# A first token tile's latent attention dealt into the expert groups of the second

## The chip, the cores and the metric

The kernel runs on one core of a Trainium2 chip. The metric is the time of one execution on the device in microseconds (us), all inputs starting in HBM. The core has TensorE (PE in the profile; PEld is its weight load), VectorE (DVE), ScalarE (ACT), GpSimd (POOL) and SyncE (SP), which run independently and wait for one another on semaphores. Each takes its own instructions in order. SP and POOL here mostly issue DMAs; one memory, SBUF, holds the tiles, and TensorE writes its sums to PSUM, eight banks of 128 x 512 fp32.

## The reference

Two transformer blocks run on 256 tokens of width 1024, all in fp32. Block one is adaptive normalisation, a mixer (gated linear attention beside sliding-window attention) and PEER, a layer of 16,384 experts of one neuron each. Block two is a latent attention (DSA), an MLP, shared keys and values, a sparse attention and a second MLP. The change concerns PEER and DSA:

```python
# PEER, for each token: 8 heads x 16 experts
s1, s2 = q1 @ keys_1.T, q2 @ keys_2.T                 # 128 scores each
v1, i1 = top_k(s1, 16); v2, i2 = top_k(s2, 16)
sc, ci = top_k(v1[:, None] + v2[None, :], 16)         # 16 of 256 pairs
experts, gates = e1 * 128 + e2, softmax(sc)
a = gelu(h . u_tab[experts])                          # one dot of 1024 per expert
out = sum(gates * a * v_tab[experts])                 # weighted rows of 1024
x = rms_norm(x + gate2 * out, final_g)                # end of block one
# DSA, on h = rmsnorm(x, g_attn)
c_q, c_kv, k_idx, w_idx = split(h @ w_in)             # 256, 128, 64, 8 columns; three normed
score = sum_h w_idx[h] * relu(q_idx[h] . k_idx)       # causal
sel = top_k(score, 64)
logits = q_abs . c_kv[sel] + rel_bias;  p = softmax(logits)
x = x + (p @ c_kv[sel]) @ w_uv @ w_o
```

A token tile is 128 tokens; causal order means that the first tile's queries see only the first tile's keys, and the second's see both.

## The kernel before

**Weights.** `weight_order` lists the big weight matrices in tiles of 128 x 1024 in the order of their use. `fetch` issues their loads on SP into a ring of four raw tiles; `prefetch` splits each into two fp32r parts, hi (ACT, line 94) and lo (DVE, line 255), and a product of split operands is three matmuls (`mm3`, lines 260 to 262, and `moving_step`, line 314). `whole_weight` hands out a raw tile unsplit, for an fp32 matmul, which the profile records as two. A second ring, `big`, is there from the latent attention on.

**Experts** (`experts`, lines 732 to 832). The two token tiles have eight groups each, one per head, a group being 16 experts for every one of 128 tokens. For each expert slot `gather` (line 743) issues an indirect DMA on POOL that brings 128 rows of 8 KB, u and v of one expert per token, into one of ten `uv` tiles. DVE takes the dot of u with h (line 815), ACT the gelu (819), DVE multiplies by the gate (805), ACT makes a diagonal matrix of the weights (753), and TensorE adds diagonal times v into two PSUM banks (755). Gelu, weights and outputs go in batches of four slots; a batch is weighed two slots after its last dot. The routing of group n + 1 (`route`, 15 steps on DVE) is dealt into the slots of group n, and all 16 gathers of group n + 1 are put into POOL's queue at slot 8 of group n (slot 0 of the first), where they wait for free tiles. The gate row gate2, a product of eight tiles of `w_gate2`, is made at the start; its eight loads (line 768) use four `uv` tiles, and the 16 query weight tiles run between.

**Latent attention** (lines 1011 to 1246) starts when both token tiles are through the experts. `block_end` forms x + gate2 * out for four halves (lines 348, 349), transposes it, splits it with the norm's gain (189, 190) and multiplies by `a_w_in`. `latents` norms the latents, transposes them, and forms the absorbed query weight from `a_w_uq` and `a_w_uk` (1021). Then come query projections (1157), index scores (1176 to 1182), eight rounds of maximum and replace for each query tile (1187, 1188), the threshold (1190), logits with the bias (1201, 1203), softmax (`add_max` 992, 980, 987), transposes, values (1227), heads (1234), and the product with `a_w_o`, three matmuls per pair (314), added to x (333). The order of the last part is the string of line 1243. DVE and ACT are kept in program order in the experts and in the first part (`manual_schedule`).

Of the kernel before, what the change touches and what calls it, by code (L numbers as in the profile page):

```python
# [26 lines left out]
EXPERT_TILES = 10  # L27
ROUTED = 8
# [4 lines left out]
def weight_order():  # L33
# [3 lines left out]
    o += [("w_out", (k,), 1024) for k in W_OUT_ORDER] + [("w_peer_q", (j,), 1024) for j in range(16)]  # L37
    mlp = lambda l: ([("w_up", (l, j), 1024) for j in range(32)] + [("w_down", (l, k), 1024) for k in range(32)])
    o += [("a_w_in", (k,), 912) for k in range(4)] + [("a_w_o", (k,), 1024) for k in range(8)] + mlp(0)
# [6 lines left out]
class Kernel:  # L46
# [7 lines left out]
    def __init__(self, ctx, tc, ins):  # L54
# [12 lines left out]
        self.first_big = [p[:2] for p in self.order].index(("a_w_o", (1,)))  # L67
# [19 lines left out]
    def prefetch(self, count, later=None):  # L87

        self.fetch(count)
        while len(self.made) < min(self.used + count, len(self.order)):  # L90
            (pool, raw), self.raw[len(self.made)] = self.raw[len(self.made)], None
            hi, lo = (pool.tile([P, 1024], F32R, name=f"w_{s}", tag=f"w_{s}", bufs=3) for s in ("hi", "lo"))
            cols = raw.shape[-1]
            self.nc.scalar.copy(hi[:, :cols], raw)  # L94
# [16 lines left out]
    def whole_weight(self, name, *idx):  # L111

        n = self.used
        assert self.order[n][:2] == (name, idx) and len(self.made) == n, (self.order[n], name, idx)
        self.fetch(1)
        (_, w), self.raw[n] = self.raw[n], None
        self.made.append(None)
# [614 lines left out]
    def experts(self, pool, gpool, hT, h_nat):  # L732
# [5 lines left out]
        junk = pool.tile([P, D], F32, name="expert_junk")  # L738
        po = {}

        def gather(idx, s):
            uv = pool.tile([P, 2 * D], F32, name="uv", tag="uv", bufs=EXPERT_TILES)
            nc.gpsimd.indirect_dma_start(out=uv, out_offset=None, in_=uv_rows,  # L743
                                         in_offset=bass.IndirectOffsetOnAxis(ap=idx[:, s:s + 1], axis=0))
            return uv

        def outputs(tt, first, last, uvs, w):

            if first:
                po[tt] = [self.ps() for _ in range(2)]  # L750
            for i, uv in enumerate(uvs):
                d = pool.tile([P, P], F32, name="diag_w", tag="diag_w", bufs=4)
                nc.scalar.activation(d, self.ident, AF.Copy, scale=w[:, i:i + 1])  # L753
                for h in range(2):
                    nc.tensor.matmul(po[tt][h], d, uv[:, D + h * 512:D + (h + 1) * 512], start=first and i == 0,  # L755
                                     stop=last and i == len(uvs) - 1)

        with tc.manual_schedule(engines={mybir.EngineType.DVE, mybir.EngineType.Activation, mybir.EngineType.Pool}):
            queries, route = self.route(pool, hT)
            groups = [(tt, h) for tt in range(2) for h in range(8)]  # L760
            routes = {0: route(*groups[0])}
            rows, sums = [], [self.ps() for _ in range(2)]
            spread = pool.tile([P, 2 * D], F32, name="uv", tag="uv", bufs=EXPERT_TILES)[:, :D].rearrange("p (k t) -> p k t", t=P)
            nc.scalar.copy(spread, self.c_cols[:, :, None].to_broadcast([P, KC, P]))
            for k in range(0, KC, 2):
                t = pool.tile([P, 2 * D], F32, name="uv", tag="uv", bufs=EXPERT_TILES)
                for i in range(2):
                    nc.sync.dma_start(t[:, i * D:(i + 1) * D], ins["w_gate2"][k + i])
                rows.append(t)
                if k < 6:  # L770
                    next(queries)

            def gate_products(k):
                for i in range(2):
                    for h in range(2):
                        nc.tensor.matmul(sums[h], spread[:, k + i], rows[k // 2][:, i * D + h * 512:i * D + (h + 1) * 512],  # L776
                                         start=(k + i == 0), stop=(k + i == KC - 1))

            for _ in routes[0][1]:
                pass  # L780
            uvs = {0: [gather(routes[0][0]["idx"], s) for s in range(SLOTS)]}
            routes[1] = route(*groups[1])
            for n in range(4):
                next(queries)
                gate_products(2 * n)
                for _ in itertools.islice(routes[1][1], 0 if n < 2 else 4):
                    pass
            for n, _ in enumerate(routes[1][1]):
                if n % 4 == 3:
                    next(queries)  # L790
            for n in range(len(groups)):
                more = n + 1 < len(groups)
                if n and more:
                    routes[n + 1] = route(*groups[n + 1])
                tt = groups[n][0]
                state, a = routes[n][0], pool.tile([P, SLOTS], F32, name="expert_a", bufs=3)
                act = pool.tile([P, SLOTS], F32, name="expert_act", bufs=3)
                w = pool.tile([P, SLOTS], F32, name="expert_w", bufs=3)
                mine = uvs.pop(n)
                starts = [0, 4, 8, 10, 12, 13, 14, 15] if not more else [0, 4, 8, 12]  # L800
# [3 lines left out]
                def weigh(c):  # L804
                    nc.vector.tensor_tensor(out=w[:, c], in0=act[:, c], in1=state["gate"][:, c], op=ALU.mult)  # L805
                    outputs(tt, n % 8 == 0 and c.start == 0, n % 8 == 7 and c.stop == SLOTS, mine[c], w[:, c])

# [786 lines left out]
```

## Time and profile before

| | us |
|---|---|
| median of three runs (lowest to highest) | 1507.04 (1505.14 to 1511.24) |
| the profiled execution | 1506.71 |
| its span, first to last instruction | 1504.9 |
| first gather issued | 179.16 |
| last dot of the experts ends | 886.4 |
| last addition of the latent attention ends | 978.6 |
| TensorE busy, over the span | 1312.5 (87%) |
| VectorE busy | 977.9 (65%) |
| ScalarE busy | 567.8 (38%) |
| GpSimd busy | 322.6 (21%) |

An engine's busy time says how long it worked, not whether anything waited for it. The span divides by what limits it: up to some 155 us the mixer, to 886 the experts, to 979 the latent attention, then MLP, sparse attention and MLP. The granted clock (PEclk) is TensorE's, as a share of 2.4 GHz, averaged over the stretch. In a row of a stretch the times stand in the order PE, PEld, DVE, ACT, POOL, each with its number of instructions, then PEclk, the share of time that the 16 DMA engines were busy, and GB/s.

### The profile page before, as it was taken

Reading aid. Unit: us, or ns where it says so; the run is one execution under the profiler, and the core shown is the slowest. Engines: PE = TensorE matmul, PEld = TensorE weight load, DVE = VectorE, ACT = ScalarE, POOL = GpSimd, SP = SyncE. Lnnn points to the kernel's source line nnn. Section 1 sums busy time; section 2 is a strip of 40 time slices with the busy share of each in tenths; the row PEclk is TensorE's granted clock in tenths of the full one; section 3 lists DMA queues with packets and bytes.
Section 4 is the critical chain, followed back from the end, with each engine's and each line's share of the span. In section 5 each row is a group of like instructions: output and inputs, shape, how many; then the busy total and the mean of one; then the engine's idle time right before and its main releaser. Section 6 shows DMA issues by size and latency. Waiting matters only on the chain.

```text
span 1504.9 us, 17588 instructions
## 1 busy us (share of the span) xinstructions
PE 1312.5 (87%) x5972; PEld 909.2 (60%) x5972; DVE 977.9 (65%) x2107; ACT 567.8 (38%) x1093; POOL 322.6 (21%) x282
## 2 busy tenths in 40 slices
PE   5999898777877777877787798999999999999998
PEld 5887784333333333323332356699988898799886
DVE  5798765666667666666666557666545777566543
ACT  2544542222222221222222146565434565465432
POOL 0001214444544445434443430000000000000000
PEclk9999999789889899888988899999999999999999
DMA  9867799999999999999999980455555582255550
GB/s 359 304 203 271 269 366 355 400 402 399 383 408 413 410 408 405 381 392 392 409 364 401 414 319 33 168 171 187 186 185 175 182 280 84 99 183 185 190 170 28
DMA packets 83653, 426.41 MB, mean 283 GB/s; under 512 B 10171, under 2 KB 13036, under 8 KB 50668
## 3 DMA queue, kind: packets, MB, share of 16 engines
q0 software_dynamic: 36864, 268.45, 44.2%
q1 hardware_dynamic: 45372, 154.74, 30.1%
q10 hardware_dynamic: 1328, 2.10, 0.4%
q8 instruction: 48, 0.79, 0.2%
q14 instruction: 41, 0.34, 0.1%
HBM read 422.63 MB, written 2.62 MB: 283 GB/s over the span
## 4 chain that ended last, share of the span: by engine, by line
PE 47%; DMA 16%; issue 16%; DVE 9%; POOL 9%; ACT 2%; POOLq 0%; SPq 0%; DVEq 0%; ACTq 0%
PE ps L314 16%; DMA uv<-in_peer_uv,idx 15%; POOL uv L743 8%; PE ps L260 7%; PE ps L262 7%; PE ps L261 7%; DVE expert_junk L815 3%; PE ps L755 3%; PE ps L410 2%; PE ps L776 1%; POOL rstd_r L138 1%; PE ps L1397 1%; DMA w_raw<-in_w_in_a 1%; PE ps L590 1%; DVE w_lo L255 1%
## 5 line engine op out<-in xcount | busy, mean ns | idle before, releaser
L755 PE MATMUL ps<-uv,diag_w 128*128 128x512 f32 x1024 | 515.4, 666 | 148.4 <-ACT diag_w L753 148.3
L755 PEld LDWEIGHTS ps<-uv,diag_w 128*128 128x128 f32 x1024 | 215.2, 215 | 447.3 <-issue 257.4
L815 DVE SCALAR_TENSOR_TENSOR expert_junk<-uv,h_nat 128x1024 f32<-128x1024 f32 x256 | 313.2, 1223 | 213.0 <-DMA uv<-in_peer_uv,idx 212.7
L255 DVE TENSOR_TENSOR w_lo<-w_raw,w_hi 128x1024 fp32r<-128x1024 f32 (+1 forms) x220 | 268.2, 1222 | 212.0 <-ACT w_hi L94 211.9
L743 POOL DMA_INDIRECT uv<-in_peer_uv,idx x256 | 302.1, 1180 | 419.0 <-PE ps L755 340.8
L94 ACT CAST w_hi<-w_raw 128x1024 fp32r<-128x1024 f32 (+1 forms) x220 | 230.0, 1049 | 261.5 <-PE ps L314 141.7
L260 PE MATMUL ps<-hT_hi,w_hi 128*128 128x256 f32 x728 | 207.3, 287 | 1.1 <-ACT hT_hi L189 1.0
L261 PE MATMUL ps<-hT_lo,w_hi 128*128 128x256 f32 x728 | 205.5, 283 | 1.0 <-DVE hT_lo L190 1.0
L262 PE MATMUL ps<-hT_hi,w_lo 128*128 128x256 f32 x728 | 204.5, 281 | 0.0
L753 ACT ACTIVATE diag_w<-ident,expert_w 128x128 f32<-128x128 f32 x256 | 87.3, 393 | 275.0 <-DVE expert_w L805 224.7
L261 PEld LDWEIGHTS ps<-hT_lo,w_hi 128*128 128x128 f32 x728 | 137.4, 189 | 3.6 <-DVE hT_lo L190 2.2
L260 PEld LDWEIGHTS ps<-hT_hi,w_hi 128*128 128x128 f32 x728 | 136.6, 188 | 3.5 <-ACT hT_hi L189 1.9
L262 PEld LDWEIGHTS ps<-hT_hi,w_lo 128*128 128x128 f32 x728 | 137.5, 189 | 0.2 <-DVE w_lo L255 0.2
L819 ACT ACTIVATE expert_act<-expert_a 128x4 f32<-128x4 f32 (+2 forms) x68 | 13.9, 205 | 228.6 <-DVE expert_junk L815 228.5
L314 PE MATMUL ps<-w_hi,u_lo 128*128 128x512 f32 x256 | 81.9, 396 | 0.0
L314 PE MATMUL ps<-w_lo,u_hi 128*128 128x512 f32 x256 | 81.7, 395 | 0.0
L314 PE MATMUL ps<-w_hi,u_hi 128*128 128x512 f32 x256 | 81.6, 395 | 0.0
L138 POOL TENSOR_TENSOR rstd_r<-fin_ms,mhalf 128x1 f32<-128x1 f32 x2 | 1.5, 739 | 326.5 <-DVE fin_ms L1476 326.5
L138 POOL TENSOR_TENSOR rstd_r<-x_ms,mhalf 128x2 f32<-128x2 f32 (+1 forms) x4 | 3.3, 835 | 293.3 <-DVE x_ms L158 293.3
L314 PEld LDWEIGHTS ps<-w_hi,u_lo 128*128 128x128 f32 x256 | 48.2, 188 | 11.4
L314 PEld LDWEIGHTS ps<-w_lo,u_hi 128*128 128x128 f32 x256 | 48.1, 188 | 11.5
L314 PEld LDWEIGHTS ps<-w_hi,u_hi 128*128 128x128 f32 x256 | 47.9, 188 | 11.4
(346 smaller groups left out, 1583.4 us busy)
## 6 DMA issues: line engine op xcount, KB each, us to landing
w_raw<-in_w_up SPq DMA_DIRECT2D x64, 512.0 KB, 3.4
w_raw<-in_w_down SPq DMA_DIRECT2D x64, 512.0 KB, 3.3
w_ada<-in_w_ada SPq DMA_DIRECT2D x40, 512.0 KB, 5.7
w_raw<-in_w_peer_q SPq DMA_DIRECT2D x16, 512.0 KB, 9.4
w_raw<-in_cmp_w SPq DMA_DIRECT2D x16, 512.0 KB, 4.1
w_raw<-in_b_w_in SPq DMA_DIRECT2D x9, 512.0 KB, 5.4
w_raw<-in_w_in_a SPq DMA_DIRECT2D x8, 512.0 KB, 9.0
w_raw<-in_w_in_m SPq DMA_DIRECT2D x8, 512.0 KB, 7.8
```

The costliest lines, as they stand in the source:

```text
L94: self.nc.scalar.copy(hi[:, :cols], raw)
L138: self.nc.gpsimd.tensor_tensor(out=r[:, :n], in0=v, in1=self.mhalf[:, :n], op=ALU.pow)
L255: return self.nc.vector.tensor_tensor(out=lo, in0=src, in1=hi.bitcast(F32), op=ALU.subtract)
L260: nc.tensor.matmul(out, lhsT[0], rhs[0], start=start, stop=False)
L261: nc.tensor.matmul(out, lhsT[0], rhs[1], start=False, stop=False)
L262: nc.tensor.matmul(out, lhsT[1], rhs[0], start=False, stop=stop)
L314: self.nc.tensor.matmul(p[tt][h], x[a][:, tt * P:(tt + 1) * P], w[b][:, h * 512:(h + 1) * 512], start=(kk == 0 and a == 0 and b == 0), sto ...
L410: nc.tensor.matmul(out[j // 2][:, j % 2], w[:, j * P:(j + 1) * P], f, start=(k == 0 and j % 2 == 0), stop=(k == KC - 1 and j % 2 == 1))
L743: nc.gpsimd.indirect_dma_start(out=uv, out_offset=None, in_=uv_rows, in_offset=bass.IndirectOffsetOnAxis(ap=idx[:, s:s + 1], axis=0))
L753: nc.scalar.activation(d, self.ident, AF.Copy, scale=w[:, i:i + 1])
L755: nc.tensor.matmul(po[tt][h], d, uv[:, D + h * 512:D + (h + 1) * 512], start=first and i == 0, stop=last and i == len(uvs) - 1)
L815: nc.vector.scalar_tensor_tensor(junk, mine[s][:, :D], 1.0, h_nat[:, tt], op0=ALU.mult, op1=ALU.mult, accum_out=a[:, s:s + 1])
```

## The change

Nine `uv` tiles instead of ten; the dot is written over the u half of its own tile. A group is weighed in batches of two (the last group ends in single slots), each at the slot after its second dot. Gathers are issued one at a time: nine at the start, then one behind each dot. Routing is no longer tied to the next group: `advance` does one and two steps per slot in turn, through all 16 groups, and a group's index and gate tiles are kept (16 each). The `w_gate2` tiles, `a_w_uq` and `a_w_uk` go through the weight ring unsplit; the absorbed weight is formed in group 1.

Once all groups are routed (`n >= 8 and not waiting`), the routing's memory is given back and `latent_tile(0, ...)`, a generator of some 40 steps that does the whole latent attention of one token tile up to the heads, is advanced one step per slot. `latent_tile(1, ...)` runs after the experts, and between its steps `fill` puts the first tile's product with `a_w_o` (`latent_out`). That product is fp32 with whole weights, loaded into tiles of their own (`wo`). The gain of the norm is put into the two parts of `a_w_in` (`gained_parts`), which is therefore loaded and split once per token tile; the product x * final_g moves from POOL to DVE. The big ring is opened after the latent attention.

```diff
-EXPERT_TILES = 10
-ROUTED = 8
+EXPERT_TILES = 9
+WHOLE = ("w_in_a", "w_gate2", "a_w_uq", "a_w_uk")
...
+    o += [("w_gate2", (k,), 1024) for k in range(8)] + [("w_peer_q", (j,), 1024) for j in range(2, 16)]
+    o += [("a_w_uq", (i,), 1024) for i in range(2)] + [("a_w_uk", (), 1024)]
-    o += [("a_w_in", (k,), 912) for k in range(4)] + [("a_w_o", (k,), 1024) for k in range(8)] + mlp(0)
+    o += [("a_w_in", (k,), 912) for _ in range(2) for k in range(4)] + mlp(0)
...
+    def gained_parts(self, raw, hi, lo, k):
+        for kk in range(2):
+            s, g = slice(kk * 456, (kk + 1) * 456), self.end_gain[:, 0, k + kk:k + kk + 1]
+            self.nc.scalar.activation(hi[:, s], raw[:, s], AF.Copy, scale=g)
+            self.nc.vector.scalar_tensor_tensor(lo[:, s], raw[:, s], g, hi[:, s].bitcast(F32), op0=ALU.mult, op1=ALU.subtract)
...
+            def advance(count=1000, upto=len(groups)):
+                while count and len(routed) < upto:
+                    state, steps = waiting[0]
+                    if next(steps, "end") == "end":
+                        waiting.pop(0)
+                        routed.append(state)
+                    else:
+                        count -= 1
...
+            for _ in range(2):
                 next(queries)
+            sums = [self.ps() for _ in range(2)]
+            for k in range(KC):
+                w = self.whole_weight("w_gate2", k)
+                for h in range(2):
+                    nc.tensor.matmul(sums[h], spread[:, k], w[:, h * 512:(h + 1) * 512], start=(k == 0), stop=(k == KC - 1))
+            advance(upto=1)
+            for _ in range(EXPERT_TILES):
+                gather()
...
-                starts = [0, 4, 8, 10, 12, 13, 14, 15] if not more else [0, 4, 8, 12]
+                starts = [0, 2, 4, 6, 8, 10, 12, 13, 14, 15] if final else list(range(0, SLOTS, 2))
...
+                if n >= 8 and shadow is None and not waiting:
+                    front.close()
+                    shadow = shadow_of(po[0], gate2)
                 for s in range(SLOTS):
                     if n == 0:
                         next(queries, None)
+                    if n == 1 and s == 4:
+                        absorbed()
+                    if final and s == 4:
+                        self.prefetch(3)
+                    if shadow is not None:
+                        next(shadow, None)
+                    else:
+                        advance(1 + s % 2)
+                    if weighed < len(batches) and batches[weighed].stop <= s:
+                        weigh(batches[weighed])
+                        weighed += 1
+                    u = uvs[n * SLOTS + s][:, :D]
+                    nc.vector.scalar_tensor_tensor(u, u, 1.0, h_nat[:, n // 8], op0=ALU.mult, op1=ALU.mult,
                                                    accum_out=a[:, s:s + 1])
...
+                    if len(uvs) < total:
+                        advance(upto=len(uvs) // SLOTS + 1)
+                        gather()
...
+            wo = [self.load(opool, ins["a_w_o"][k], [P, D], f"a_w_o{k}") for k in range(KC)]
+            self.fetch(4)
+            out0, out1 = self.latent_out(0, wo), self.latent_out(1, wo)
+            for _ in self.latent_tile(1, x_mid, po, gate2, h_nat[:, 0], lambda n: list(itertools.islice(out0, n))):
+                pass
+            for _ in out0:
+                pass
+            self.prefetch(2)
+            for _ in out1:
+                pass
...
+    def latent_tile(self, tt, x_old, po, gate2, final_g, fill=lambda n: None):
...
+            for h, s in halves:
+                self.gated_add(pool, xp[:, s], xp[:, s], po[h], gate2[:, s])
+                for k in range(4):
+                    nc.tensor.transpose(ps[h][:, k], xp[:, (4 * h + k) * P:(4 * h + k + 1) * P], self.ident)
+                yield
...
+            for h, s in halves:
+                self.split(ps[h], hT[0][:, 4 * h:4 * h + 4], hT[1][:, 4 * h:4 * h + 4])
+                yield
+                for k2 in range(2 * h, 2 * h + 2):
+                    hi, lo = self.weight("a_w_in", k2, last=True)
...
+            rn, rx = self.power(ms, 1), self.power(var, 1)
+            yield
...
+            nc.vector.tensor_scalar(sl, sl, eps, None, op0=ALU.add)
+            r = self.power(sl, 3)
+            yield
...
+            for _ in range(8):
+                m8 = self.small.tile([P, 8], F32, name="idx_m8")
+                nc.vector.max(out=m8, in_=keep)
+                nc.vector.match_replace(out=keep, in_to_replace=m8, in_values=keep, imm_value=-3e38)
+                yield
...
+                yield from softmax(0)
+                yield
+                transposed(0, nc.scalar.copy)
+                yield from softmax(4)
+                fill(1)
+                yield
+                values(0)
+                fill(1)
+                yield
+                heads_out(0, nc.scalar.copy)
+                transposed(4, nc.vector.tensor_copy)
...
+    def latent_out(self, tt, wo):
+        p = [self.ps() for _ in range(2)]
+        steps = itertools.product(range(KC), range(2)) if tt == 0 else ((c, h) for h in range(2) for c in range(KC))
+        for c, h in steps:
+            self.nc.tensor.matmul(p[h], self.oT[:, c, tt * P:(tt + 1) * P], wo[c][:, h * 512:(h + 1) * 512],
+                                  start=(c == 0), stop=(c == KC - 1))
```

## Rows read from the trace of the kernel before

**Rows 1.** Stretches: us; busy us (instructions) by engine; PEclk, DMA share, GB/s.
```profile
155.00:262.00 107.00, 101.12 (x564) 74.04 (x562) 69.88 (x154) 42.11 (x78) 28.05 (x25) 0.97 0.88 342
262.00:874.00 612.00, 467.53 (x922) 194.92 (x923) 402.98 (x1018) 132.63 (x349) 273.18 (x231) 0.87 0.99 399
...
886.00:979.00 93.00, 84.54 (x400) 64.83 (x399) 64.60 (x194) 53.71 (x118) 8.28 (x8) 0.98 0.34 121
```

**Rows 2.** The page's chain that ended last, shares by engine.
```profile
PE 47%; DMA 16%; issue 16%; DVE 9%; POOL 9%; ACT 2%; POOLq 0%; SPq 0%; DVEq 0%; ACTq 0%
```

**Rows 3.** Groups by form, 270 to 870 us: busy, mean ns | idle.
```profile
L755 PE MATMUL ps<-uv,diag_w 128*128 128x512 f32 x911 | 462.8, 670 | 137.9 <-ACT diag_w L753 137.8
L815 DVE SCALAR_TENSOR_TENSOR expert_junk<-uv,h_nat 128x1024 f32<-128x1024 f32 x228 | 279.0, 1223 | 196.4 <-DMA uv<-in_peer_uv,idx 196.2
L743 POOL DMA_INDIRECT uv<-in_peer_uv,idx x227 | 269.1, 1185 | 336.9 <-PE ps L755 294.2 <-issue 13.8 <-DVE expert_junk L815 8.4
```

**Rows 4.** Waits, 262 to 874 us: total us, times, longest.
```profile
POOL uv L743 <- PE ps L755: 296.1, 153, 10.1
...
DVE expert_junk L815 <- DMA uv<-in_peer_uv,idx: 198.2, 179, 3.5
```

**Rows 5.** Timeline of GpSimd: start, duration, operation [idle before].
```profile
262.09 1.78 POOL L743 DMA_INDIRECT uv<-in_peer_uv,idx  x1 [0.76 <-PE ps L755]
...
873.98 0.94 POOL L743 DMA_INDIRECT uv<-in_peer_uv,idx  x1 [0.38 <-PE ps L755]
```

**Rows 6.** DMA queues (packets, MB, share) and issues (count, us to landing).
```profile
q0 software_dynamic: 36864, 268.45, 44.2%
...
uv<-in_peer_uv,idx POOLq DMA_INDIRECT x256, 9.8
```

**Rows 7.** The chain by time: start, us, what; two TensorE runs.
```profile
172.07 3.43 PE ps L776 x8
...
963.87 13.36 PE ps L314 x57
```

**Rows 8.** Stretches, columns as in the first group: a well supplied one, two clocks.
```profile
480.00:520.00 40.00, 30.73 (x63) 12.48 (x61) 27.01 (x69) 7.93 (x21) 17.42 (x16) 0.88 1.01 417
...
861.00:865.00 4.00, 3.95 (x5) 1.85 (x6) 2.10 (x3) 0.88 (x3) 0.00 (x0) 0.50 1.02 424
865.00:889.00 24.00, 24.00 (x57) 10.48 (x56) 11.86 (x26) 5.97 (x19) 6.75 (x6) 0.99 0.94 375
```

**Rows 9.** Timeline of SyncE's DMA issues: start, duration, what.
```profile
208.37 10.69 SPq L84 DMA_DIRECT2D w_raw<-in_a_w_in  x4
...
234.56 0.43 SPq L967 DMA_DIRECT2D bias<-bias_dram  x1
...
814.56 0.43 SPq L123 DMA_DIRECT2D wqi<-in_a_w_q_idx  x1
```

**Rows 10.** Groups by form in the tail, 886 to 979 us.
```profile
L255 DVE TENSOR_TENSOR w_lo<-w_raw,w_hi 128x1024 fp32r<-128x1024 f32 x13 | 15.5, 1222 | 9.9 <-ACT w_hi L94 9.9
...
L314 PE MATMUL ps<-w_hi,hT_hi 128*128 128x512 f32 x32 | 11.5, 419 | 0.0
...
L190 DVE SCALAR_TENSOR_TENSOR hT_lo<-ps,end_gain,hT_hi 128x256 fp32r<-128x256 f32 x8 | 3.8, 481 | 3.5 <-ACT hT_hi L189 3.5
```

**Rows 11.** Timeline of VectorE, the ends of the tail's stages.
```profile
885.18 1.23 DVE L815 SCALAR_TENSOR_TENSOR expert_junk<-uv,h_nat 128x1024 f32<-128x1024 f32 x1 [1.85 <-DMA uv<-in_peer_uv,idx]
...
906.91 0.63 DVE L1025 COPY lat_raw<-ps 128x456 f32<-128x456 f32 x1 [1.73 <-PE ps L262]
...
913.31 0.69 DVE L1052 COPY latT<-ps 128x512 f32<-128x512 f32 x1 [0.62 <-PE ps L1051]
...
927.08 0.62 DVE L1187 MAX8 idx_m<-score 128x8 f32<-128x128 f32 x2
...
936.47 0.42 DVE L1190 TENSOR_SCALAR score<-score 128x128 f32<-128x128 f32 x2
...
977.94 0.69 DVE L333 TENSOR_TENSOR x_res<-x_res,ps 128x512 f32<-128x512 f32 x1 [0.71 <-PE ps L314]
```

More of the change, by code (lines that the diff above doesn't have):

```diff
@@ L93, in prefetch @@
             cols = raw.shape[-1]
+            if name == "a_w_in":
+                self.gained_parts(raw, hi, lo, 2 * idx[0])
+                self.made.append((hi, lo))
+                continue
             self.nc.scalar.copy(hi[:, :cols], raw)
@@ L729, in swa_steps, with experts, gather @@
             yield
-    def experts(self, pool, gpool, hT, h_nat):
+    def experts(self, pool, gpool, front, hT, h_nat, absorbed, shadow_of):
         nc, ins, tc = self.nc, self.ins, self.tc
         uv_rows = ins["peer_uv"]
-        junk = pool.tile([P, D], F32, name="expert_junk")
         po = {}
-        def gather(idx, s):
+        groups = [(tt, h) for tt in range(2) for h in range(8)]
+        total = len(groups) * SLOTS
+        uvs = []
+        rp = front.enter_context(tc.tile_pool(name="routes", bufs=1, reuse_waits="tile"))
+        def gather():
+            n, s = divmod(len(uvs), SLOTS)
@@ L765, in experts @@
[L765 to L777, printed above, removed]
@@ L791, in experts @@
-            for n in range(len(groups)):
[L792 to L799, printed above, removed]
-                starts = [0, 4, 8, 10, 12, 13, 14, 15] if not more else [0, 4, 8, 12]
+            queries, route = self.route(rp, pool, hT)
@@ new lines, in experts @@
+            for _ in range(2):
+                next(queries)
+            sums = [self.ps() for _ in range(2)]
[6 more added lines that the diff above has]
+                gather()
+            for n in range(5):
+                next(queries)
+                advance(0 if n < 3 else 4, 2)
@@ new lines, in run @@
+        with pool("rows", side="right") as rows:
+            po, gate2 = self.experts(rows, gpool, front, hT, h_nat, lambda: self.absorbed(w_abs), begin)
+        with pool("a_w_o", side="right") as opool, tc.manual_schedule(
+                engines={mybir.EngineType.DVE, mybir.EngineType.Activation}):
+            wo = [self.load(opool, ins["a_w_o"][k], [P, D], f"a_w_o{k}") for k in range(KC)]
[7 more added lines that the diff above has]
+            for _ in out1:
+                pass
@@ L1237, in weights_ready @@
-            def weights_ready(n):
-                with tc.issue_after(done[n].ins), tc.issue_after(projected.ins):
-                    self.prefetch(5)
-            ops = {"S": softmax, "T": transposed, "V": values, "U": heads_out, "W": lambda n: next(steps), "P": weights_ready}
-            steps = self.moving_steps("a_w_o", range(KC), oT, self.add_to_x)
-            for o in "S1 T1 S0 V1 T0 S3 V0 U0 S2 P0 T3 W0 V3 T2 W1 V2 W2 U4 W3".split():
-                ops[o[0]](int(o[1]))
-            for _ in steps:
-                pass
+                        nc.vector.scalar_tensor_tensor(keep, rl[:, i], widx[:, h:h + 1], prev, op0=ALU.mult, op1=ALU.add)
@@ new lines, in latent_tile @@
+                        prev = keep
+                    yield
+            for h0 in (0, 4):
+                nc.scalar.activation(qa[:, h0:h0 + 4], proj(self.w_abs, h0), AF.Copy, scale=float(128.0 ** -0.5))
+                yield
+            for i in range(8):
+                nc.tensor.matmul(logits[i], qa[:, i], latT[:, 2, :S], start=False, stop=(i % per == per - 1))
+            fill(2)
+            yield
+            for _ in range(8):
+                m8 = self.small.tile([P, 8], F32, name="idx_m8")
+                nc.vector.max(out=m8, in_=keep)
+                nc.vector.match_replace(out=keep, in_to_replace=m8, in_values=keep, imm_value=-3e38)
+                yield
@@ new lines, in latent_out @@
+    def latent_out(self, tt, wo):
[4 more added lines that the diff above has]
+                                  start=(c == 0), stop=(c == KC - 1))
+            if c == KC - 1:
+                if tt == 0 and h == 0:
+                    continue
+                for i in range(2) if tt == 0 else (h,):
+                    self.add_to_x(tt, i, p[i])
+            if h == 1 or tt:
+                yield
```

450 lines of the change are left out of this document (192 added, 258 removed).

## The prediction

> **What bounds the kernel now.** I read the stages first [rows 1]. From 262 to 874 us the DMA engines are busy 0.99 of the time at 399 GB/s, while TensorE is at 468 of 612 us and VectorE at 403: this stage, the gathers of the experts, is bound by the transfers. From 886 to 979, the latent attention, the DMA share is 0.34 and no engine is full: a chain of dependent steps. What comes after it, the two MLPs and the sparse attention, the change doesn't touch. The chain that ended last [rows 2] says the same over all: PE 47%, DMA 16%, issue 16%. Within the experts [rows 3] one expert costs VectorE a dot product of 1.22 us, GpSimd an issue of 1.19 us and TensorE four records (two fp32 matmuls, each recorded twice). The waits [rows 4] close a circle: GpSimd waits 296 us for TensorE to free a row tile, VectorE 198 us for gathered rows. Whether the circle or the transfers set the pace is the question of the first half below.
>
> **The gather stream.** From 262 to 874 us GpSimd issues 231 gathers [rows 1], the first of them, the 26th of all, at 262.09, the last, the 256th, at 873.98 [rows 5]: 230 pitches in 611.9 us, 2.66 us each. Ten tiles at that pitch mean that a tile comes round every 26.6 us; 9.8 us of it are issue to landing [rows 6], so a tile is held 16.8 us. That is the batch of four: its first tile waits for three more landings, two more dots and the matmuls. With pairs, I sum: half a pitch for the partner (1.3), the dot (1.3 with its accumulator read), activation, weighting and diagonal (some 1.0), on average 2.6 us of matmuls (four records of 0.43 [rows 7] for the first of a pair, eight for the second), and the issue (1.2): 7.4, say 8 us. Nine tiles at a pitch of 2.5 us leave 22.5 - 8 = 14.5 us for the transfer, against 9.8: the queue is fuller with nine tiles than before with ten, and the transfers alone set the pace. What pace? In the best long stretch, 480 to 520 us, the share is 1.01 and the rate 417 GB/s [rows 8]. A gather is 268.45 MB / 256 = 1.049 MB [rows 6], so 2.51 us; at the mean 399 GB/s it is 2.63. I take 2.53, nearer the stretch that was well supplied; bounds 2.49 and 2.60 for the forecast.
>
> By the Trainium skill (DMA: Bandwidth & Descriptors, Where 436 GB/s comes from) some 358 GB/s of HBM per core bind a load, and no reordering would help. The trace shows 399 over 612 us, so the measurement decides against it; by that page the pitch would not fall, which is the first rival.
>
> Other loads in that stretch: before, lat_g and wqi at 814 us (0.23 and 0.52 MB, in the pitch of 2.66) [rows 9]. a_w_in (1.87 MB) and the bias (1.05) went at 208 and 235 us, before the stretch, the rest after it. Now the stretch carries a_w_in twice (3.74), bias 1.05, final_g, wuv and c_causal (1.17), lat_g and wqi (0.75): 6.7 MB, 16 us at 415 GB/s. So 230 x 2.53 + 16 = 598 us instead of 612: **-14 us**.
>
> **Up to the 26th gather** I take no change, -5 to +8 us. TensorE is 101 of 107 us busy there [rows 1]: the same 16 query tiles, gate products and 16 experts have to pass it. For a gain: the first routing stands behind two query tiles instead of three, and has no weight splits of VectorE in front of it. For a loss: the eight w_gate2 loads had tiles of their own and went at once; now they share four ring tiles, and on SP's queue the query weights stand behind them, so TensorE can wait a few us for a landing. The absorbed weight product and its three loads (1.6 MB) move here from the end.
>
> **Cover for the dealt steps.** Routing now takes 24 steps per group against 15 per group needed, so it is finished after group 8, and tile 0's some 40 steps fill 40 slots of groups 9 to 11. VectorE per slot without routing: 1.31 for the dot, 0.08 for its half of a weighting; of 2.53 us 1.14 are free, 46 us in 40 slots. The tail before has 64.6 us of VectorE [rows 1], of which 15.5 are weight splits [rows 10]; half of the rest, some 25, plus eight gained splits of some 0.65 (456 columns; 256 take 0.48, [rows 10]) is 30 us: it fits. TensorE: 84.5 us less 33 of the output product (three groups of matmuls as the one in [rows 10]), halved, 26 us; free are 40 x (2.53 - 1.72) = 32. That is tight, and I allow 0 to +6 us. Two steps use GpSimd's power, which stands in its queue behind a gather that waits for a tile; VectorE then waits for it with the next weighting behind it, some 4 us each time. 14 us of landed or flying rows cover that. The 16 extra VectorE instructions of the second a_w_in split (four us in one go in the last group) fall where nine tiles are in flight: nothing. Writing the dot over its own operand instead of a scratch tile: the same instruction, nothing.
>
> **The tail.** The last dot ends at 886.4 and the last addition to x at 978.6, 92.2 us [rows 11]. Stage by stage for one token tile:
> Dots to input product: before 20.5 us (to 906.9). Now 2.4 until the sums are out, two gated adds 2.7, transposes, splits 1.4 each, 24 matmuls of 0.205 instead of 48 and one late gained split: 10.8.
> To the transposed latents: before 7.1 (to 914.0); without the two raw copies and one of two powers, but with the squares of x behind the split: 5.5.
> To the first maximum: before 13.1 (to 927.08), VectorE on 16 score updates; now 8 of 0.5 us behind half the projections: 8.5.
> Eight rounds and the threshold: before 9.8; now only the 256 wide half, 8 x 0.73 + 0.3: 6.1.
> From there to the last addition: before 41.7, most of it 96 matmuls of 0.234 [rows 7]. The whole fp32 product has 64 records of 0.43, 27.5 us against 22.4. Two of tile 0's eight steps lie beside the rounds, six (10.3 us) in the softmax, and tile 1's 13.8 stand alone at the end. With some 7 us of values, transposes and heads on TensorE, 5.5 us until the softmax gives it work and 0.9 for the last addition: 37.5.
> Sum 68.4 against 92.2: **-24 us**. The bounds are -12 (banks of PSUM: four hold logits, two the output, so two are left to rotate and the chain waits for copies) and -29. The whole a_w_o (4.2 MB) loads from the moment the row tiles come free, some 10 us, and is wanted after about 25: hidden. With that cover gone it would cost what it is late. The MLP starts with two prepared tiles; 0 to +2 us.
>
> **Sum.** The profiled execution took 1506.71 us (span 1504.9), the median of the runs is 1507.04, so I add to the former: -14 + 0 - 24 = -38, **1469 us**.
>
> **Rivals.**
> (1) The stream doesn't get faster: 0.99 of DMA share says that it is full already. Then 612 + 14 us for 6.0 MB more, less 24: 1497. Against it: share 1.01 goes with 417 GB/s, 0.99 with 399 [rows 1, 8].
> (2) TensorE's clock swings. After 6.6 us idle it was at 0.50 (1.2 GHz) from 861 to 865, and at 0.99 (2.4 GHz) once it worked through [rows 8]. Pairs give bursts of 3.4 us with 1.6 us between. If it were low half of the time, an expert would cost 2.57 us, 190 of them 8 us more, and 40 slots with tile 0's work 3.1, 22 more: 1499. For it: mean clock 0.87 with the bursts of four. Against it: the gaps get shorter than those that preceded a fall. The Trainium skill (TensorE: Matmul & The Clock Gate, A second HAM failure mode: psum-queue depth-cycling) has a kernel whose short pauses between groups made the clock swing; no row here shows it with gaps so short.
> (3) Slower: nine tiles run dry. If a tile is still held 15 us, because its release stands behind VectorE's order (routing or dealt step, dot, weighting) and TensorE's, then (9.8 + 15) / 9 = 2.76 us of pitch, 230 x 2.76 + 16 = 651, +39 - 24 = +15: 1522. It decides against the change from a pitch of 2.70, a hold of 14.5 us. For it: one tile fewer, and more on VectorE per slot in both halves. Against it: pairs cut the hold by itself, and VectorE still idles 198 us for rows [rows 4].
>
> **Chances.** Forecast 0.62, (1) 0.14, (2) 0.08, (3) 0.12, something else 0.04. The forecast's own range is 1452 to 1487 (pitch -9 and +16, start -5 and +8, tail -5 and +12, not all at once); with (1) and (2) the range is 1452 to 1500. Half a per cent, 7.5 us, is about what a measurement of this kernel tells from no change: faster means under 1499.5. Nearly all of the forecast, most of (1) and half of (2): 0.79 faster, 0.08 the same, 0.13 slower.
>
> **What would show it.** The issue of the 256th gather near 860 us, with no pauses of 6 us in groups 1 to 8; a DMA rate of 415 GB/s or more; TensorE's clock nearer 1 in the experts; the last dot near 872 us; the dealt steps between some 600 and 710 us with the pitch there under 2.7; a tail of 68 us that ends in 14 us of output product. I am wrong if the rate stays at 400 GB/s (rival 1), if the granted clock falls under 0.8 (rival 2), or if gathers wait for tiles while the DMA share drops (rival 3).

## The result, and the profile after

The changed kernel takes 1483.57 us (median of four runs, 1481.97 to 1487.59), against 1508.99 for the kernel before on the same chip: a ratio of 0.984, 95% interval 0.981 to 0.987. It is some 25 us (1.6%) faster, where 38 were forecast; the time lies in the range. The profiled execution is the 1481.97 us one, with a span of 1480.2.

First the stretches of the changed kernel, columns as in [rows 1]:

```profile
155.00:276.00 121.00, 108.27 (x588) 77.97 (x587) 81.83 (x219) 44.35 (x88) 31.45 (x26) 0.99 0.84 318
276.00:586.00 310.00, 231.26 (x492) 90.03 (x490) 253.22 (x735) 91.33 (x234) 131.27 (x124) 0.98 1.01 421
586.00:735.00 149.00, 127.18 (x366) 63.30 (x367) 91.84 (x227) 49.03 (x140) 62.56 (x57) 0.94 0.97 387
735.00:889.00 154.00, 113.61 (x241) 44.85 (x240) 81.63 (x156) 30.31 (x96) 52.88 (x54) 0.97 0.99 410
889.00:956.00 67.00, 61.87 (x240) 36.68 (x239) 33.93 (x95) 25.97 (x61) 1.95 (x3) 0.97 0.25 92
```

The steady stream (second line) is full: 421 GB/s at a share of 1.01, with a clock of 0.98 against 0.87 in [rows 1]. The stretch with tile 0's steps (third) falls to 387, and the start (first) has 318 where it had 342, although it is 14 us longer. GpSimd's gathers put times to that, the 9th, 10th, 26th and 256th (start, duration, [idle before]; before: [rows 5]):

```profile
184.92 0.94 POOL L767 DMA_INDIRECT uv<-in_peer_uv,idx  x1 [0.31 <-issue]
222.99 0.98 POOL L767 DMA_INDIRECT uv<-in_peer_uv,idx  x1 [37.13 <-PE ps L780]
...
275.64 1.60 POOL L767 DMA_INDIRECT uv<-in_peer_uv,idx  x1 [4.08 <-PE ps L780]
...
869.80 0.95 POOL L767 DMA_INDIRECT uv<-in_peer_uv,idx  x1 [0.71 <-PE ps L780]
```

And VectorE the last dot and the ends of the tail's stages (transposed latents, first maximum, threshold, last addition), which answer to [rows 11]:

```profile
887.86 1.23 DVE L846 SCALAR_TENSOR_TENSOR uv<-uv,h_nat 128x1024 f32<-128x1024 f32 x1 [0.80 <-DMA uv<-in_peer_uv,idx]
...
904.65 0.42 DVE L1167 COPY latT<-ps 128x256 f32<-128x256 f32 x1 [0.69 <-ACT latT L1166]
...
913.56 0.43 DVE L1208 MAX8 idx_m<-score 128x8 f32<-128x256 f32 x1
...
921.43 0.29 DVE L1211 TENSOR_SCALAR score<-score 128x256 f32<-128x256 f32 x1
...
955.71 0.69 DVE L351 TENSOR_TENSOR x_res<-x_res,ps 128x512 f32<-128x512 f32 x1 [6.18 <-PE ps L1268]
```

From these lines and the rows of before, the 25 us by stage:

| | before | after | difference | forecast |
|---|---|---|---|---|
| up to the 26th gather | 262.1 | 275.6 | +13.6 | 0 |
| from there to the end of the last dot | 624.3 | 613.5 | -10.9 | -14 |
| last dot to last addition | 92.2 | 67.3 | -24.9 | -24 |
| from there to the end | 526.3 | 523.8 | -2.5 | 0 |
| span | 1504.9 | 1480.2 | -24.7 | -38 |

The page's chain that ended last has moved towards the DMA, 23% against 16% in [rows 2]:

```profile
PE 45%; DMA 23%; DVE 12%; issue 10%; POOL 6%; ACT 3%; POOLq 0%; SPq 0%; DVEq 0%; ACTq 0%
```

The start is nearly the whole miss. Why it grew, what the dealt steps cost, and whether the pairs made the stream faster is what the experiments ask. Their ratios are to the kernel before on the same chip, whose median was 1501 to 1508 us; between experiments of different chips the ratios and the stages of the traces count, not the times alone.

### The profile page after: what moved, and what is told of

Read it like the earlier page. It is cut to its first block, busy times and chain, and to the rows that moved or that the text cites. A ratio compares the mean times of both kernels' runs of the same rounds, so it can differ in the third digit from the quotient of the medians.

```text
span 1480.2 us, 17835 instructions
## 1 busy us (share of the span) xinstructions
PE 1289.0 (87%) x6004; PEld 884.5 (60%) x6004; DVE 981.3 (66%) x2166; ACT 582.8 (39%) x1165; POOL 292.3 (20%) x280
## 4 chain that ended last, share of the span: by engine, by line
PE 45%; DMA 23%; DVE 12%; issue 10%; POOL 6%; ACT 3%; POOLq 0%; SPq 0%; DVEq 0%; ACTq 0%
DMA uv<-in_peer_uv,idx 21%; PE ps L332 14%; PE ps L278 6%; PE ps L280 6%; PE ps L279 6%; POOL uv L767 5%; DVE uv L846 4%; PE ps L780 3%; PE ps L428 2%; DMA w_raw<-in_w_peer_q 2%; PE ps L1268 1%; PE ps L806 1%; DVE w_lo L273 1%; POOL rstd_r L156 1%; DVE ada_junk L376 1%
## 5 line engine op out<-in xcount | busy, mean ns | idle before, releaser
L780 PE MATMUL ps<-uv,diag_w 128*128 128x512 f32 x1024 | 484.2, 620 | 130.3 <-ACT diag_w L778 130.3
L780 PEld LDWEIGHTS ps<-uv,diag_w 128*128 128x128 f32 x1024 | 191.6, 196 | 411.3 <-ACT diag_w L778 211.8
L846 DVE SCALAR_TENSOR_TENSOR uv<-uv,h_nat 128x1024 f32<-128x1024 f32 x256 | 312.6, 1223 | 125.2 <-DMA uv<-in_peer_uv,idx 121.7
L273 DVE TENSOR_TENSOR w_lo<-w_raw,w_hi 128x1024 fp32r<-128x1024 f32 x208 | 254.1, 1224 | 196.1 <-ACT w_hi L104 193.1
L767 POOL DMA_INDIRECT uv<-in_peer_uv,idx x256 | 276.1, 1079 | 442.1 <-PE ps L780 284.4
L104 ACT CAST w_hi<-w_raw 128x1024 fp32r<-128x1024 f32 x208 | 217.9, 1050 | 266.4 <-PE ps L332 122.9
L850 ACT ACTIVATE expert_act<-expert_a 128x2 f32<-128x2 f32 (+1 forms) x130 | 26.5, 203 | 393.1 <-DVE uv L846 393.0
L332 PEld LDWEIGHTS ps<-w_lo,u_hi 128*128 128x128 f32 x256 | 48.1, 188 | 10.9
```

The costliest lines, as they stand in the source:

```text
L273: return self.nc.vector.tensor_tensor(out=lo, in0=src, in1=hi.bitcast(F32), op=ALU.subtract)
L332: self.nc.tensor.matmul(p[tt][h], x[a][:, tt * P:(tt + 1) * P], w[b][:, h * 512:(h + 1) * 512], start=(kk == 0 and a == 0 and b == 0), sto ...
L780: nc.tensor.matmul(po[tt][h], d, uvs[n * SLOTS + s][:, D + h * 512:D + (h + 1) * 512], start=n % 8 == 0 and s == 0, stop=n % 8 == 7 and s ...
L846: nc.vector.scalar_tensor_tensor(u, u, 1.0, h_nat[:, n // 8], op0=ALU.mult, op1=ALU.mult, accum_out=a[:, s:s + 1])
L850: nc.scalar.activation(act[:, c], a[:, c], AF.Gelu)
```

## Experiments

**1. The loads of w_gate2 at the start** (`a_gate_rows`)

```diff
-                w = self.whole_weight("w_gate2", k)        # eight tiles through the weight ring
...
+                t = pool.tile([P, 2 * D], F32, name="uv", tag="uv", bufs=EXPERT_TILES)
+                for i in range(2):
+                    nc.sync.dma_start(t[:, i * D:(i + 1) * D], ins["w_gate2"][k + i])
...
+                if n < 4:
+                    gate_products(2 * n)                   # between the query tiles
```

> The changed kernel, with the eight w_gate2 tiles loaded into four free uv tiles at the start and their products dealt between the query tiles, as in the kernel before. Supply theory (the start lost 13.6 us because the w_gate2 loads fill the weight ring: from 155 to 175 us only 113 and 252 GB/s flow, and the query weights then share the DMA with the first nine gathers): the 26th gather moves from 275.6 to 264 to 268 us, the last dot from 889 to 879 to 881, the time from 1483.6 to about 1475. TensorE theory (the absorbed product, 4.6 us, and one more expert before the 26th gather, 2.9 us, fill TensorE, and the order of the loads doesn't matter): the 26th gather stays at 273 to 277 us, the time at 1482 to 1485.

Measured 1472.2 us, ratio 0.978 (0.975 to 0.981), against 0.984 for the changed kernel; 26th gather at 266.61, 9.0 us earlier, last dot over at 879.6, 9.5 us earlier. The first stretches show why: those of the changed kernel,

```profile
155.00:165.00 10.00, 9.32 (x67) 7.95 (x66) 5.96 (x15) 5.53 (x9) 0.00 (x0) 1.00 0.37 113
165.00:175.00 10.00, 10.00 (x25) 4.50 (x24) 7.47 (x29) 0.50 (x3) 1.17 (x2) 1.00 0.72 252
```

and those of this one:

```profile
155.00:165.00 10.00, 9.25 (x69) 8.40 (x67) 9.18 (x13) 8.16 (x14) 0.00 (x0) 0.88 0.89 345
165.00:175.00 10.00, 9.89 (x63) 7.98 (x63) 8.19 (x33) 4.37 (x8) 0.00 (x0) 1.00 0.72 287
```

In the ring of four, a w_gate2 tile keeps its place until TensorE has used it, and the query weights behind it on SP wait. The numbers of the supply theory came, those of the TensorE theory did not. The edit also deals the products with w_gate2 between the query tiles; what that does without the loads was not tried.

**2. The start of the kernel before** (`start2`: as 1, and ten query tiles ahead of the first dot, no routing in group 0, the absorbed weight in group 4)

```diff
...
-                    if n == 1 and s == 4:
+                    if n == 4 and s == 4:
                         absorbed()
...
-                    else:
+                    elif n:
                         advance(1 + s % 2)
```

> The changed kernel with the start of the kernel before: w_gate2 in free uv tiles, ten query tiles ahead of the first dot instead of eight, no routing step dealt into group 0, and the absorbed query weight formed in group 4 instead of group 1. By the supply and the TensorE theory together: the 26th gather at 254 to 260 us (266.6 with the w_gate2 tiles alone, 275.6 in the changed kernel), the last dot at 868 to 873, the time at 1461 to 1467. If the ten tiles of the kernel before made its start (rival): the 26th gather stays at 265 to 268, the time at 1471 to 1474.

Ratio 0.977 (0.973 to 0.980): 1471.5 us. The 26th gather came at 256.95, as expected, but the last dot only at 877.3, 2.3 us before that of experiment 1: a miss. Here is the 26th gather of experiment 1, and that of this kernel:

```profile
266.61 1.43 POOL L766 DMA_INDIRECT uv<-in_peer_uv,idx  x1 [2.68 <-PE ps L779]
...
256.95 0.94 POOL L766 DMA_INDIRECT uv<-in_peer_uv,idx  x1 [0.97 <-PE ps L779]
```

From the 26th gather to the last dot it took 620.3 us instead of 613.0, and 255.1 MB landed in that time instead of 252.2: 2.9 MB more, 6.9 us at 421 GB/s. Of these, 2.2 MB are gathered rows that had been asked for earlier and were still on their way, the rest other loads (three tiles of a_w_in are issued from 259 us on instead of from 241; the absorbed weight's loads stayed in the start, at 205 to 213 us). From 155 us to the last dot both kernels move some 290 MB at 401 GB/s. A gather issued earlier is worth something only if the DMA engines would have idled.

**3. The query tiles dealt** (`best4`: as 2, with 5 and the following edit)

```diff
-                    if n == 0:
+                    if (n * SLOTS + s) % 3 == 0:
                         next(queries, None)     # and five steps ahead of the first dot instead of ten
```

> best2 with the query tiles dealt: five of their steps ahead of the first dot instead of ten, the rest one in every third slot until they are through (group 2), and the absorbed weight in group 5. TensorE theory of the start (in best2 it is busy 106 of 110 us from 155 to 265 while the DMA share falls to 0.71 to 0.91 between 215 and 255, because the released tiles wait for query tiles): the first dots come 10 to 15 us sooner, the 26th gather at 243 to 252 us instead of 261, the last dot 5 to 10 us sooner (865 to 870), the time 1456 to 1462. Bytes theory (rival: the query weights move from the start into the stream, 1.25 us each, and what is won ahead of the 26th gather is paid behind it, as start2 showed): the last dot within 3 us of 875, the time 1464 to 1468.

1454.8 us, ratio 0.969 (0.964 to 0.974), the shortest time of all. The 26th gather came at 250.43, as the TensorE theory expected, and the last dot is over at 863.6, like the time a little under that theory's range, and 11.8 us before that of `best2` (experiment 5), which differs in this and in forming the absorbed weight one group earlier. The two ran on different chips: by the ratios (`best2` 0.973) the gap is some 7 us, and the intervals overlap. In `best2` the start still had stretches like these,

```profile
215.00:225.00 10.00, 10.00 (x70) 8.53 (x69) 4.38 (x6) 2.63 (x7) 1.92 (x2) 1.00 0.91 363
225.00:235.00 10.00, 9.57 (x59) 7.33 (x57) 4.03 (x9) 1.77 (x6) 1.87 (x2) 1.00 0.71 248
```

and here they are full:

```profile
215.00:225.00 10.00, 10.00 (x48) 6.57 (x47) 4.21 (x8) 1.70 (x7) 3.65 (x4) 1.00 1.02 418
225.00:235.00 10.00, 10.00 (x40) 5.87 (x40) 7.27 (x12) 3.99 (x9) 4.52 (x4) 1.00 1.02 421
```

TensorE is as busy in both; what differs is that the expert products no longer stand behind query tiles which nobody needs yet. From 155 us to the last dot both move 290 MB, `best2` at 403 GB/s and `best4` at 410. So the start was bound by TensorE's order as well as by the ring, and the bytes theory, right in experiment 2, fails here because these bytes fill time that had been idle.

**4. Tile 0 not dealt** (`e_undealt`)

```diff
-                    if shadow is not None:
-                        next(shadow, None)
-                    else:
+                    if shadow is None:
                         advance(1 + s % 2)
```

> The changed kernel, with no step of tile 0's latent attention dealt into the groups: all of it runs after the last dot, ahead of tile 1's. If dealing hides tile 0's chain at a price of some 12 us of the stream: the dip from 586 to 735 us is gone, the last dot comes at 876 to 881, and the tail grows by tile 0's chain up to the heads, 40 to 50 us as tile 1's takes from 889 to 941: time 1513 to 1525. If the deal only moves the cost (rival): the time is within 8 us of 1483.6.

1518.6 us, ratio 1.010 (1.007 to 1.013): 1% slower than the kernel before. The dip is gone,

```profile
586.00:735.00 149.00, 111.46 (x238) 43.57 (x239) 77.47 (x148) 26.69 (x89) 56.33 (x59) 0.99 1.01 421
```

the last dot is over at 877.3, and the last addition ends at 992.2, a tail of 114.9 us. The deal costs 11.8 us ahead of the last dot, 10.8 of them behind the 26th gather (613.5 us to the last dot against 602.7), and takes 47.6 out of the tail. Some 5 of the 10.8 are loads that fall behind the last dot here: one a_w_in and three w_up tiles, 2 MB. That leaves some 6 us for the dealt steps themselves.

**5. Waits in the dealt steps** (`c2_spaced`; `best2` is 2 with this)

```diff
             r = self.power(sl, 3)
-            yield
+            for _ in range(5):
+                yield
...
-                nc.scalar.copy(qi, proj(self.wqi, 0))
+                p = proj(self.wqi, 0)
+                yield
+                yield
+                nc.scalar.copy(qi, p)          # the same for absorbed queries, values and heads
```

> The changed kernel, with empty slots put between a producer and its consumer in the dealt steps: five slots instead of one from the power of the latent norms to its use, and two between a TensorE product and the ACT or DVE copy of it (query projections, absorbed queries, values, heads). Order theory (the dip to 387 GB/s from 586 to 735 us comes from waits in program order: VectorE 7.8 us for a power that stands on GpSimd behind a gather waiting for a tile, and 5.1, 5.4, 4.0 and 5.0 us for ACT or TensorE, whose queue holds a copy of a product that is not there yet): the stretch returns to 410 GB/s or more, the last dot comes 7 to 11 us earlier (878 to 882), the time is 1473 to 1476. TensorE theory (it is full from 650 to 680 us, so the dealt products themselves cost the stream): the last dot stays within 3 us of 889, the time at 1481 to 1485.

> The start of the kernel before (as in start2) and the spaced steps (as in c2_spaced) together. If the two losses are separate, they add up: some 4 us under start2, last dot at 863 to 869, time 1456 to 1463. If the later start of the dealt steps makes the second cost what the first gains (rival): no more than 1 us under start2.

In the changed kernel VectorE idles in the dip like this, for GpSimd's power, for the gelu, and for a product. Below them are the waits of ScalarE (total us, times, longest) for products that it was to copy, with the next gelu behind the copy:

```profile
631.34 1.13 DVE L1158 SCALAR_TENSOR_TENSOR lat<-ps,rstd_r,lat_g 128x256 f32<-128x256 f32 x4 [7.79 <-POOL rstd_r L156]
...
642.14 0.16 DVE L825 TENSOR_TENSOR expert_w<-expert_act,gate 128x2 f32<-128x2 f32 x1 [5.09 <-ACT expert_act L850]
...
658.98 0.16 DVE L825 TENSOR_TENSOR expert_w<-expert_act,gate 128x2 f32<-128x2 f32 x1 [5.41 <-ACT expert_act L850]
...
708.74 0.69 DVE L1240 COPY oT<-ps 128x512 f32<-128x512 f32 x1 [5.04 <-PE ps L1239]
...
ACT q_abs L1200 <- PE ps L1177: 6.0, 2, 4.2
ACT q_idx L1183 <- PE ps L1177: 5.9, 1, 5.9
...
ACT oT L1240 <- PE ps L1239: 4.2, 1, 4.2
```

With the spacing VectorE's waits over 2 us (those for gathered rows left out), eight in that stretch before, are two (3.1 and 2.5, both for the exponentials of the softmax), and the stretch recovers:

```profile
586.00:735.00 149.00, 124.32 (x364) 60.93 (x363) 95.02 (x231) 48.33 (x139) 68.77 (x59) 0.95 1.00 409
```

The time is 1479.2 us, ratio 0.983 (0.980 to 0.986), whose interval overlaps that of the changed kernel. The last dot (887.35) lies within 3 us of 889, as the TensorE theory had it, but the start was 2 us later here (26th gather at 277.69). From there to the end of the last dot it takes 609.7 us against 613.5, and 602.7 undealt: 3.8 us won, of 7 to 11 expected and of the 6 or so that the dealt steps cost. The order theory has the cause of most of that price, as far as single traces tell, but had the price too high. `best2` came to 1467.1 us (0.970 to 0.977), 4.4 below `start2`, as much as the spacing gives by itself; its absolute range was missed because that of `start2` was.

**6. Which part made the stream faster** (the kernel before with both edits, `h_before_pairs`, or with the second alone, `i_before_lag1`; `d_fours`: the changed kernel with batches of four and with four more empty slots behind one power)

```diff
 # h_before_pairs
-                starts = [0, 4, 8, 10, 12, 13, 14, 15] if not more else [0, 4, 8, 12]
+                starts = [0, 2, 4, 6, 8, 10, 12, 13, 14, 15] if not more else list(range(0, SLOTS, 2))
 # h_before_pairs and i_before_lag1
-                    while weighed < len(batches) and (s == SLOTS - 1 or batches[weighed].stop + (2 if more or s < 8 else 0) <= s + 1):
+                    while weighed < len(batches) and (s == SLOTS - 1 or batches[weighed].stop + (1 if more or s < 8 else 0) <= s + 1):
```

> The kernel before, with one part of the change alone: weighed in batches of two instead of four, one slot after the second dot instead of two; ten tiles, sixteen gathers at once, and the latent attention as before. Hold theory (a tile was held 16.8 us of its 26.6 us round because a batch of four waits for its last landing; with pairs some 8 to 9 us): the pitch falls from 2.66 to 2.48 to 2.55 us, the rate rises from 399 to 412 to 421 GB/s, the granted clock from 0.87 to 0.95 or more, the last dot from 886 to 850 to 862, the time from 1507 to 1472 to 1484. Rival (the gain of the stream came from gathers issued one by one and routing spread over all slots): pitch 2.60 or more, clock under 0.92, time 1495 or more.

> The changed kernel, weighed in batches of four instead of two (one slot after the last dot of a batch), with four more empty slots behind the power of the latent norms so that GpSimd's queue can't lock. Hold theory: a tile is held some 16 us as in the kernel before, nine tiles give (9.8 + 16) / 9 = 2.87 us of pitch, 230 x 0.38 = some 85 us more than the changed kernel's 2.49: 1560 to 1580, with the clock back under 0.92. If the stream owes its rate to gathers issued one by one and not to the pairs (rival): pitch under 2.6, time under 1510.

> The kernel before, with batches of four as they were, but each weighed one slot after its last dot instead of two. It divides the gain of the stream between the size of the batch and the wait behind it. Pairs (the two-slot lag is a small part of the hold of 16.8 us): hold some 14 us, rate 400 to 408 GB/s, 1492 to 1503 us. Lag (with four in a batch and one slot of lag, nine tiles gave 416 GB/s in d_fours): hold 11 to 13 us, rate 414 to 420 GB/s, 1477 to 1490 us.

`h_before_pairs` took 1475.2 us, ratio 0.980 (0.978 to 0.983), as the hold theory had it. But `d_fours`, expected at 1560 to 1580, took 1489.6 (0.984 to 0.992), only some 6 us more than with pairs, with its 26th gather 5.0 us later (280.68). And `i_before_lag1`, the kernel before with a single 2 made a 1, took 1473.8, ratio 0.983 (0.978 to 0.987): 27 us less, as much as the whole change, and it keeps ten tiles and sixteen gathers issued at once: the rival of `d_fours`, gathers issued one by one, isn't what the stream needed. The last dot is over at 855.1 in h and 852.2 in i (886.4 before). From 262 to 840 us h shows

```profile
262.00:840.00 578.00, 433.06 (x916) 171.63 (x917) 398.75 (x1052) 144.59 (x400) 258.15 (x227) 0.97 1.01 421
```

and i

```profile
262.00:840.00 578.00, 455.90 (x921) 188.38 (x920) 395.76 (x995) 126.67 (x343) 278.92 (x230) 0.90 1.01 418
```

Both also come to the 26th gather sooner than the kernel before, whose time was 262.09; h first:

```profile
253.45 0.94 POOL L743 DMA_INDIRECT uv<-in_peer_uv,idx  x1 [0.31 <-PE ps L755]
...
253.65 0.94 POOL L743 DMA_INDIRECT uv<-in_peer_uv,idx  x1 [0.31 <-PE ps L755]
```

The medians from issue to landing are, for h, i, d and the changed kernel:

```profile
uv<-in_peer_uv,idx POOLq DMA_INDIRECT x256, 16.4
...
uv<-in_peer_uv,idx POOLq DMA_INDIRECT x256, 11.5
...
uv<-in_peer_uv,idx POOLq DMA_INDIRECT x256, 11.1
...
uv<-in_peer_uv,idx POOLq DMA_INDIRECT x256, 15.3
```

Working the hold as in the prediction (tiles times pitch, here 1.049 MB over the steady rate, less that median): h 10 x 2.49 - 16.4 = 8.5, i 10 x 2.51 - 11.5 = 13.6, d 9 x 2.52 - 11.1 = 11.6, the changed kernel 9 x 2.49 - 15.3 = 7.1, against 16.8 before. So the slot of lag behind a batch was enough to starve the queue, and without it batches of four fill it too. Pairs shorten the hold further, for a queue that is already full, and keep the clock higher (0.97 against 0.90) without a use for it.

**7. Eight tiles** (`g_eight`)

```diff
-EXPERT_TILES = 9
+EXPERT_TILES = 8
```

> The changed kernel with eight uv tiles instead of nine. Hold theory: 8 x 2.49 - 8 = 11.9 us are left for the transfer, more than the 9.8 it needs, so the rate in the steady stretch (276 to 586 us) stays at 415 to 421 GB/s; the dealt steps, whose stalls of 5 to 8 us had a deeper queue to draw on, lose 3 to 8 us more: 1484 to 1493. If the hold is nearer 12 us (rival): steady rate under 405 GB/s and 1500 or more.

1490.3 us, ratio 0.988 (0.984 to 0.992), in the expected range. The steady rate is 419 GB/s, the dip 370:

```profile
276.00:586.00 310.00, 231.53 (x487) 90.33 (x486) 252.02 (x736) 92.21 (x235) 130.91 (x122) 0.97 1.01 419
586.00:735.00 149.00, 121.50 (x354) 60.15 (x352) 88.34 (x220) 46.50 (x132) 58.81 (x55) 0.94 0.94 370
```

A tile less costs almost nothing in steady flow; it costs where a wait has to be bridged.

## Why the prediction was right, and where it was not

**Gather stream: right in the mechanism.** The hold forecast for pairs ("7.4, say 8 us") came out at 7.1 and 8.5, and in the steady stretch the transfers set the pace at 2.49 us, the lower bound given, instead of the 2.53 chosen. "That is the batch of four" was half wrong: of its "three more landings, two more dots", experiment 6 shows that taking the lag of one slot away is enough, and the landings could have stayed. Because the new kernel removes both, the sum didn't show the error. The sum also went by pitches between issues, and let the last dot follow the 256th gather by 12 us as before ("near 860", "near 872"). It followed by 19.3 (869.80 to 889.09), in a queue where a gather takes 15.3 us to land instead of 9.8; roughly, the other kernels go with it (13.7 us in i at 11.5, 21.3 in h at 16.4).

**Other loads: right in size, in part by luck.** Behind the 26th gather the queue of SP's loads moved 6.5 MB up to the last dot, against 1.9 before; the forecast had 6.7 MB against 0.75. But they are not the loads that it named. The first a_w_in and the bias were issued ahead of the 26th gather, at 231 to 271 us; three w_up tiles and the first of a_w_o, which the term had not, came in ahead of the last dot.

**Cover for the dealt steps: a price at the upper end of the allowance, and nothing for it in the sum.** "0 to +6 us" was allowed, and the sum took 0; experiment 4 puts some 6 us on the steps themselves, beside 5 of loads. It named TensorE as the tight engine; the waits that show are in program order (the power behind gathers, as foreseen but 7.8 us instead of 4; and ACT's copies of products that are not there yet, ahead of the gelu, not foreseen). "14 us of landed or flying rows cover that" held for one wait, not for eight: the stretch fell to 387 GB/s. The better pitch paid for part of all this, so the errors left -10.9 against -14: a small miss made of several larger ones, which is in part luck.

**Up to the 26th gather: the step that failed,** no change forecast, +8 as the bound, +13.6 measured. The prediction saw that "the query weights stand behind them" on SP and priced it at "a few us for a landing". The price is that of the whole queue: from 155 to 175 us 3.7 MB flowed, where 8.4 would have at 421 GB/s. Experiment 1 puts 9.0 us of the stage on it. The miss is larger than 13.6, though, for the forecast had nothing here for the batches: with nothing but a slot of lag less (i, and h with pairs as well) the kernel before reaches its 26th gather at 253.5 instead of 262.1, so the rest of the change cost some 22 us of start, of which the edits of experiments 1 and 2 together give back 19. What is left beside the loads has two sources in sight: the absorbed weight's products, 4.6 us more for TensorE (busy 107.9 of the 120.6 us from 155 to the 26th gather), and ACT in program order, as here in the changed kernel, where the gelu of a pair waits for a query tile and two table loads and VectorE's next weighting for the gelu (idle 9.20 us, to 248.91):

```profile
245.06 0.58 ACT L892 COPY pq<-ps 128x512 f32<-128x512 f32 x1 [5.59 <-PE ps L280]
245.66 1.28 ACT L929 ACT_TABLE_LOAD   x1
246.96 0.31 ACT L929 ACTIVATE gate<-best_v,gate_neg 128x16 f32<-128x16 f32 x1
247.17 0.19 ACT L929 ACTIVATION_READ_ACCUMULATOR gate<-best_v,gate_neg 128x1 f32 x1
247.38 1.28 ACT L850 ACT_TABLE_LOAD   x1
248.67 0.20 ACT L850 ACTIVATE expert_act<-expert_a 128x2 f32<-128x2 f32 x1
```

How the rest divides between these two was not tried one by one, and stays open; `best4` shows only that with the query tiles spread nothing of it is left (26th gather at 250.4).

**Tail: right, and by its stages.** 67.3 us against 68.4: to the transposed latents 16.0 (16.3 forecast), first maximum 8.5 (8.5), rounds 8.2 (6.1; a round takes 0.98 us, not 0.73), from there 34.7 (37.5). TensorE's last 13.7 us of output product stand alone at the end, as forecast.

**What comes after, forecast at 0 to +2:** -2.5 us; the cause was not looked for.

**The rivals.** (1) A stream at 399 GB/s: refuted, 421. The Trainium skill (DMA: Bandwidth & Descriptors, Where 436 GB/s comes from) lets HBM bind at some 358 GB/s, and the trace disagrees, with 421 over 310 us. The Trainium skill (Perfetto Trace Analysis, Roofline) takes some 120% of that as the practical ceiling of a core alone. That makes 430 GB/s, an estimate from this page, and the trace agrees with it. (2) The clock: it held, at 0.98 in the stream. (3) Nine tiles run dry: not in steady flow, even with eight; for some 150 us, in the dealt steps, a little.

## What to carry to other kernels

When the transfers bind a stage, count the bytes and the time in which the DMA engines idle, start included: an edit gains there only by filling idle DMA time, and the cheapest one here was a single slot of lag (286 MB from 155 us to the last dot, at 391 GB/s before and 410 with it). A load moved into a shared ring can cost what everything behind it on its queue then waits for, not only its own landing. Work dealt into a full pipeline should have slots between a producer and the in-order engine that consumes it, and work that isn't due yet (query tiles) should stand behind work that frees a buffer.

## What the runs showed of the hardware

From 276 to 586 us every kernel but two ran at 419 to 421 GB/s and a DMA share of 1.01, with eight, nine or ten tiles, in pairs or (`i_before_lag1`) in fours; `d_fours` with nine tiles ran at 416, the kernel before at 402. With ten tiles, granted clocks of 0.90 (fours) and 0.97 (pairs) gave the same rate to within 1%. Switching ACT between exponential and gelu costs a table load of 1.28 us each way, and with routing dealt between the gelus these fall into the stream.
